# Moving eight of the tail's 36 extraction matmuls into the pauses of the last sums, and decode steps behind the last masks, in a top-10 kernel

## The chip, the cores and the metric

The kernel runs on one core of one Trainium2 chip. The metric is the device time of one execution in microseconds (us). Other words used below: TensorE is the matmul engine (PE in the profile, its weight loads PEld), VectorE is DVE, ScalarE is ACT, GpSimd is POOL, SyncE is SP. "Granted clock" is the share of TensorE's full clock that the throttle let through. A "pass" is one matmul of the profile in the extraction; an "ending" is the kernel's tail, from A (in the table below) on.

## The reference

```python
def reference(x, k):                      # x: [8192, 8192] float32, k = 10
    indices = np.argpartition(x, -k, axis=1)[:, -k:]
    values = np.take_along_axis(x, indices, axis=1)
    sorted_idx = np.argsort(-values, axis=1)
    return np.take_along_axis(indices, sorted_idx, axis=1)   # int64 [8192, 10]
```

## The kernel before

There are 64 tiles of 128 rows. For each tile ScalarE writes e = exp(36(x - 4.7)) in bf16, TensorE sums e into column groups (`s`, in PSUM), VectorE finds the 16 groups with the largest sums ("choose"), GpSimd gathers the candidates of 12 of them ("gather"), VectorE and GpSimd each spread half of the candidates into a masked square ("mask"), TensorE moves them to the right rows with 12 small fp32 matmuls ("extract"; each is two passes in the profile, so 24 passes a tile), and VectorE ranks them. Every few tiles a batch is decoded into column numbers: `slot`, `low`, `hot`, `pick`, `val` on VectorE, then `rows`, which places the values for the row moves on TensorE (`fo`). For all batches but one the rows are written by VectorE; for the last but one, ScalarE writes them with 16 instructions.

The parts that the change and the argument touch (cut):

```python
    def choose_steps(t):
        ...
        early = t >= last - 1            # the last two tiles gather in two halves
        return [
            lambda: nc.vector.max(out=w16[:, 0:8], in_=m),
            lambda: nc.vector.max_index(out=cid[:, 0:8], in_max=w16[:, 0:8], in_values=m),
        ] + ([lambda: index(0, G // 2), lambda: gather(t, 0, G // 2)] if early else []) + [
            lambda: nc.vector.match_replace(out=m2, ...),
            lambda: nc.vector.max(out=w16[:, 8:16], in_=m2),
            lambda: nc.vector.max_index(out=cid[:, 8:16], ...),
        ] + ([lambda: index(G // 2, G), lambda: gather(t, G // 2, G)] if early
             else [lambda: index(0, G)])

    def mask(eng, t, g0, g1):            # two SBUF inputs, 128x768 for half a tile
        eng.tensor_tensor(out=masked[t][:, g0:g1], in0=cands[t][:, g0:g1]..., in1=layout(t).own..., op=ALU.mult)

    def extract(t, c0=0, c1=G):
        for c in range(c0, c1):
            nc.tensor.matmul(gs[t][:, c * R:(c + 1) * R], lhsT=masked[t][:, c]..., rhs=layout(t).place)

    def finish_steps(b):
        ...
        return [slot, low, hot, hot_times_cid, pick, val, spread_rows] + moves + [copy_out, dma_out]   # named here for short

        # the tail: a, b, c are the last three tiles; wc holds the sums' steps of c
        mask(nc.gpsimd, a, G // 2, G)
        run(choose_steps(b))
        mask(nc.vector, a, 0, G // 2)
        run(wc[4:])                      # the last four sums of c, with pauses for ScalarE
        run(later[1:])
        extract(a)                       # then three extractions without a pause
        run(rank_steps(a - 1))
        steps = finish_steps(batch_of[a - 1])
        run(steps[:4])
        mask(nc.gpsimd, b, G // 2, G)
        chosen = choose_steps(c)
        run(chosen[:4])
        mask(nc.vector, b, 0, G // 2)
        run(chosen[4:])
        extract(b)
        run(steps[4:7])                  # pick, val, rows of the last-but-one batch
        mask(nc.vector, c, 0, G // 2)
        extract(c, 0, G // 2)
        ...                              # good: a check of the sums
        run(rank_steps(a))
        mask(nc.vector, c, G // 2, G)
        extract(c, G // 2, G)
        run(steps[7:])                   # the row moves on TensorE
        run(rank_steps(b)); run(rank_steps(c))
        ...
        run(finish_steps(batch_of[last]))
```

## Time and profile before

| | us |
|---|---|
| three timed runs | 678.6, 679.62, 681.07 |
| profiled run | 680.31 (span on the core 678.5) |
| last exponential on ScalarE ends ("A") | 653.22 from the start of the span |
| maximum over the last sums starts on VectorE ("T") | 653.98 |
| last extraction pass ends on TensorE | 669.12 |
| last rows start on VectorE | 673.16 |

The prediction below shows the lines that carry its reading. Two things help with them. A line of the chain of waits is "start, us, what", and each was released by the one above it or by its own engine's order. In a timeline the number in brackets at the end is the engine's idle time before the group and what ended it. And one more view of before, which the prediction did not show, will matter: the timeline of VectorE ahead of the last rows.

```profile
669.15 0.37 DVE L282 MAX8 t8a<-g 128x8 f32<-128x192 f32 x1 [3.23 <-PE g L269]
...
672.86 0.19 DVE L351 SCALAR_TENSOR_TENSOR val<-low,pick 128x30 f32<-128x30 uint16 x1
673.16 0.41 DVE L317 TENSOR_TENSOR rows<-val,cpack 128x240 f32<-128x240 f32 x1
```

VectorE idles 3.23 us until TensorE has finished the extraction of c, then ranks and decodes c without a stop up to the rows. So in the kernel before the rows start 4.04 us after the last extraction pass (673.16 - 669.12) because of VectorE's own steps. The row moves on TensorE lie beside that and are done by 672.50.

### The profile page before, as it was taken

To read this page: it belongs to the slowest core of one execution; us is meant where nothing else is said; L and a number is where in the kernel's file an instruction comes from. 1 tells how busy PE (TensorE), PEld (TensorE's weight loads), DVE (VectorE), ACT (ScalarE), POOL (GpSimd) and SP (SyncE) were. 2 spreads that over 40 slices of the span, in tenths; PEclk is the share of its full clock that TensorE was granted. 3 is DMA by queue.
4 is the path that set the end of the run, shared out by engine and by line. 5 is a ranking of instruction groups with operands and counts; after the bars stand their busy time and mean duration, and the time that the engine had idled before them with its cause. 6 is when DMAs were issued, how large, how long until landed. Compare 5 with 4: busy or idle time off the path is not lost.

```text
span 678.5 us, 7906 instructions
## 1 busy us (share of the span) xinstructions
PE 549.6 (81%) x2645; PEld 343.8 (51%) x2690; DVE 552.9 (81%) x1272; ACT 495.3 (73%) x295; POOL 180.0 (27%) x136
## 2 busy tenths in 40 slices
PE   1488877887978988877987888897988988877977
PEld 0146544555634555653753555553555555554656
DVE  3568878789868988789787897888977899879985
ACT  4777777777777777776777777687777777778851
POOL 0113223313313223313322313322331322331330
PEclk9867987859866777798787685976788768788875
DMA  8999999999999999999999999999999999999910
GB/s 354 420 421 420 419 421 419 421 419 421 419 421 420 421 418 420 421 419 420 420 421 420 420 419 421 420 419 421 419 420 418 421 417 415 418 420 398 405 49 7
DMA packets 73712, 269.77 MB, mean 398 GB/s; under 512 B 4398, under 2 KB 5062, under 8 KB 73670
## 3 DMA queue, kind: packets, MB, share of 16 engines
q1 hardware_dynamic: 72976, 268.54, 97.0%
q10 hardware_dynamic: 694, 0.71, 0.3%
q8 instruction: 21, 0.34, 0.2%
q14 instruction: 21, 0.17, 0.1%
HBM read 268.58 MB, written 0.66 MB: 397 GB/s over the span
## 4 chain that ended last, share of the span: by engine, by line
DMA 61%; PE 12%; SPq 7%; ACT 7%; issue 5%; DVE 5%; POOL 3%; ACTq 0%; DVEq 0%
DMA xt<-in_x_dram 59%; SPq L115 7%; ACT e L181 7%; PE s L188 6%; PE g L269 5%; POOL cand L235 3%; DMA out_dram<-opack 2%; DVE wall L222 1%; PE fo L333 1%; DVE cidb L228 1%; DVE cidb L223 1%; DVE m L225 1%; DVE wall L227 1%; DVE masked L252 0%; DVE pick L350 0%
## 5 line engine op out<-in xcount | busy, mean ns | idle before, releaser
L181 ACT ACTIVATE e<-xt,bias 128x4096 bf16<-128x4096 f32 (+2 forms) x138 | 477.6, 3461 | 153.4 <-DMA xt<-in_x_dram 136.4
L188 PE MATMUL s<-e,group 128*128 128x512 bf16 x979 | 334.6, 496 | 122.1 <-ACT e L181 117.6
L188 PEld LDWEIGHTS <-group 128*128 128x128 bf16 x1024 | 122.1, 122 | 309.5 <-issue 254.0
L269 PEld LDWEIGHTS g<-cpack,masked 128*128 128x128 f32 x1536 | 210.7, 217 | 17.9 <-issue 5.8
L269 PE MATMUL g<-cpack,masked 128*128 128x8 f32 (+1 forms) x1536 | 202.7, 272 | 2.0 <-DVE masked L252 1.7
L235 POOL INDIRECT_COPY cand<-xt,idx 128x192 f32 (+1 forms) x66 | 65.9, 998 | 476.3 <-DMA xt<-in_x_dram 129.1
L222 DVE MAX8 wall<-s 128x8 f32<-128x1024 f32 (+1 forms) x64 | 77.2, 1206 | 113.9 <-PE s L188 105.2
L252 POOL TENSOR_TENSOR masked<-cand,cpack 128x768 f32<-128x768 f32 x63 | 113.2, 1797 | 5.2
L223 DVE FIND_INDEX8 cidb<-wall,s 128x8 uint16<-128x1024 f32 (+1 forms) x64 | 76.7, 1198 | 0.0
L228 DVE FIND_INDEX8 cidb<-wall,m 128x8 uint16<-128x1024 f32 (+1 forms) x64 | 76.4, 1193 | 0.0
L225 DVE MATCH_REPLACE8 m<-wall,s 128x1024 f32<-128x1024 f32 (+1 forms) x64 | 76.1, 1189 | 0.0
L227 DVE MAX8 wall<-m 128x8 f32<-128x1024 f32 (+1 forms) x64 | 75.8, 1184 | 0.2
L252 DVE TENSOR_TENSOR masked<-cand,cpack 128x768 f32<-128x768 f32 x65 | 61.8, 951 | 0.0
L333 PE MATMUL fo<-rows,send 128*64 128x160 f32 (+3 forms) x128 | 27.8, 366 | 1.1 <-DVE rows L317 1.1
L181 ACT ACTIVATION_READ_ACCUMULATOR e<-xt,bias 128x1 f32 x138 | 25.7, 186 | 0.0
L333 PEld LDWEIGHTS fo<-rows,send 128*64 128x64 f32 (+2 forms) x128 | 18.1, 159 | 3.3 <-DVE rows L317 1.7
L282 DVE MAX8 t8a<-g 128x8 f32<-128x96 f32 (+1 forms) x64 | 16.2, 253 | 3.3 <-PE g L269 3.2
L285 DVE FIND_INDEX8 posb<-t8a,g 128x8 uint16<-128x96 f32 (+1 forms) x64 | 16.7, 260 | 0.0
L287 DVE FIND_INDEX8 posb<-tall,g 128x8 uint16<-128x96 f32 (+1 forms) x64 | 16.4, 257 | 0.0
L283 DVE MATCH_REPLACE8 g<-t8a,g 128x96 f32<-128x96 f32 (+1 forms) x64 | 16.1, 252 | 0.0
L214 DVE TENSOR_SCALAR idx<-cidb,cpack 128x12 uint16<-128x12 uint16 (+1 forms) x66 | 15.6, 237 | 0.2
L286 DVE MAX8 tall<-g 128x8 f32<-128x96 f32 (+1 forms) x64 | 15.8, 247 | 0.0
(38 smaller groups left out, 85.8 us busy)
## 6 DMA issues: line engine op xcount, KB each, us to landing
xt<-in_x_dram SPq DMA_DIRECT2D x248, 1024.0 KB, 16.0
xt<-in_x_dram SPq DMA_DIRECT2D x15, 512.0 KB, 9.1
xt<-in_x_dram SPq DMA_DIRECT2D x2, 256.0 KB, 10.1
out_dram<-opack ACTq DMA_DIRECT2D x6, 80.0 KB, 5.1
cpack<-topk_cpack ACTq DMA_DIRECT2D x1, 141.0 KB
out_dram<-opack ACTq DMA_DIRECT2D x1, 70.0 KB
out_dram<-opack SPq DMA_DIRECT2D x1, 60.0 KB, 1.7
out_dram<-opack SPq DMA_DIRECT2D x1, 30.0 KB, 1.5
```

Of the source, the lines that this page charges most:

```text
L115: nc.sync.dma_start(out=dst[:, s:s + n, :], in_=src[:, s:s + n, :])
L181: nc.scalar.activation(out=e, in_=xts[t][:, s0 * W:(s0 + n) * W], func=ACTF.Exp, bias=bias[:, 0:1], scale=BETA, accum_out=eall[:, first_su ...
L188: nc.tensor.matmul(sums[:, j:j + BANK], lhsT=lay.group[:, s0 + i, :], rhs=e[:, i * W + j:i * W + j + BANK], start=s0 + i == 0, stop=s0 + i ...
L222: lambda: nc.vector.max(out=w16[:, 0:8], in_=m),
L223: lambda: nc.vector.max_index(out=cid[:, 0:8], in_max=w16[:, 0:8], in_values=m),
L225: lambda: nc.vector.match_replace(out=m2, in_to_replace=w16[:, 0:8], in_values=m, imm_value=-1.0),
L227: lambda: nc.vector.max(out=w16[:, 8:16], in_=m2),
L228: lambda: nc.vector.max_index(out=cid[:, 8:16], in_max=w16[:, 8:16], in_values=m2),
L235: nc.gpsimd.add_instruction(mybir.InstIndirectCopy(name=nc.get_next_instruction_name(), ins=[nc.gpsimd.lower_ap(xts[t]), nc.gpsimd.lower_a ...
L252: eng.tensor_tensor(out=masked[t][:, g0:g1], in0=cands[t][:, g0:g1].unsqueeze(2).to_broadcast(shape), in1=layout(t).own.rearrange("p (c s) ...
L269: nc.tensor.matmul(gs[t][:, c * R:(c + 1) * R], lhsT=masked[t][:, c, :, :].rearrange("p a s -> p (a s)"), rhs=layout(t).place, start=True, ...
L333: nc.tensor.matmul(fo, lhsT=lay.send[:, i, 0:n * S], rhs=rows[:, i].rearrange("p a k -> p (a k)"), start=i == 0, stop=i == n - 1)
```

## The change

The intent: (1) do 8 of the 12 extraction matmuls of a in the pauses between the last four sums, where TensorE waits for ScalarE, and not behind them; (2) put the first mask of b ahead of the last choice, where VectorE is idle; (3) keep the second mask of c from waiting behind decode steps that are not yet needed: `val` and ScalarE's `rows` go behind it. The diff is whole:

```diff
@@ -403,28 +403,30 @@
         mask(nc.gpsimd, a, G // 2, G)
         run(choose_steps(b))
         mask(nc.vector, a, 0, G // 2)
-        run(wc[4:])
+        done = 0
+        for i, n in ((4, 3), (5, 3), (6, 2), (7, 4)):
+            run(wc[i:i + 1])
+            extract(a, done, done + n)
+            done += n
 
         run(later[1:])
-        extract(a)
         run(rank_steps(a - 1))
         steps = finish_steps(batch_of[a - 1])
         run(steps[:4])
         mask(nc.gpsimd, b, G // 2, G)
-        chosen = choose_steps(c)
-        run(chosen[:4])
         mask(nc.vector, b, 0, G // 2)
-        run(chosen[4:])
         extract(b)
-        run(steps[4:7])
+        run(choose_steps(c))
         mask(nc.vector, c, 0, G // 2)
         extract(c, 0, G // 2)
+        run(rank_steps(a))
+        run(steps[4:5])
+        mask(nc.vector, c, G // 2, G)
+        extract(c, G // 2, G)
+        run(steps[5:7])
         nc.vector.tensor_scalar(
             out=good[:, 0:nsums], in0=eall, scalar1=FINITE, scalar2=None, op0=ALU.is_lt,
         )
-        run(rank_steps(a))
-        mask(nc.vector, c, G // 2, G)
-        extract(c, G // 2, G)
         run(steps[7:])
         run(rank_steps(b))
         run(rank_steps(c))
```

## The prediction

> **What bounds the kernel now.** I read the page first, then the chain of waits, then the timeline and the stretch table of the last 30 us, because the diff touches nothing but the code for the last three tiles (a, b, c in the source). The page:
>
> ```profile
> span 678.5 us, 7906 instructions
> ...
> PEclk9867987859866777798787685976788768788875
> DMA  8999999999999999999999999999999999999910
> ...
> DMA 61%; PE 12%; SPq 7%; ACT 7%; issue 5%; DVE 5%; POOL 3%; ACTq 0%; DVEq 0%
> ```
>
> The DMA engines are full for all but the last 34 us (two slices of 17 us); they stream x and the change leaves them alone. So only the part after the last bytes, about 651 to 678 us, can move. The end of the chain that ended last, in order of time (start, us, what):
>
> ```profile
> 653.36 0.58 PE s L188
> 653.94 15.17 PE g L269 x72
> 669.12 3.38 PE fo L333 x12
> ...
> 672.52 0.30 ACT opack L330
> ...
> 673.16 0.42 DVE rows L317
> ...
> 673.62 1.05 PE fo L333 x6
> ```
>
> TensorE sets the end: after the last sums it does three extractions without a pause (72 passes; an fp32 matmul of the source is two passes, 36 matmuls), then the row moves of the last-but-one batch (12 passes). The last rows on VectorE start at 673.16, and what follows is fixed: 5.3 us to the end of the span. So I forecast one number, when those rows start. The stretch table (us, busy of PE, PEld, DVE, ACT, POOL, then granted clock, DMA share, GB/s), with stretches cut where the clock changes:
>
> ```profile
> 646.50:649.91 3.41, 1.88 (x8) 0.58 (x7) 3.29 (x10) 3.33 (x7) 1.12 (x2) 1.00 0.11 43
> 649.91:653.32 3.41, 1.74 (x6) 0.48 (x5) 2.25 (x8) 3.36 (x8) 0.81 (x2) 1.00 0.09 34
> 653.32:656.74 3.42, 3.38 (x16) 3.29 (x16) 2.69 (x7) 0.00 (x0) 2.14 (x2) 0.50 0.00 0
> 656.74:660.15 3.41, 3.41 (x18) 3.41 (x18) 3.27 (x7) 0.00 (x0) 0.93 (x1) 0.50 0.00 0
> ```
>
> The clock is full until 653.32 and half to the end, although TensorE is then never idle. A pass of the extraction costs 15.38/72 = 0.214 us there. At full clock it cost 1.41/12 = 0.118 us:
>
> ```profile
> 641.54 1.41 PEld L269 LDWEIGHTS g<-cpack,masked 128*128 128x128 f32 x12 [0.49 <-DVE masked L252]
> ```
>
> The pauses that the change fills, and the other engines' steps that could become the path (timelines of PE, POOL, ACT):
>
> ```profile
> 650.67 0.59 PE L188 MATMUL s<-e,group 128*128 128x512 bf16 x2 [0.58 <-ACT e L181]
> 651.95 1.08 PE L188 MATMUL s<-e,group 128*128 128x512 bf16 x3 [0.69 <-ACT e L181]
> 653.36 0.58 PE L188 MATMUL s<-e,group 128*128 128x512 bf16 x1 [0.33 <-ACT e L181]
> ...
> 657.95 0.93 POOL L235 INDIRECT_COPY cand<-xt,idx 128x96 f32 x1 [2.40 <-DVE m L225]
> 661.56 0.64 POOL L235 INDIRECT_COPY cand<-xt,idx 128x96 f32 x1 [2.68 <-DVE masked L252]
> ...
> 660.32 3.88 ACT L322 ACTIVATE rows<-val,cpack 128x60 f32<-128x60 f32 x16 [7.01 <-DVE val L351]
> ```
>
> ScalarE writes the rows for the last-but-one batch by 664.2, and TensorE uses them at 669.05: 4.8 us of slack in the kernel before.
>
> [...]every change of the clock in it lies on one grid of 3.413 us, the last at 653.32. [...]this trace says that the fp32 extraction counts for little, since 100% busy stretches of it stay at 0.50. [...]Measured is 118 ns at full and 214 ns at half clock; [...] Here the gather starts 2.2 and 2.5 us after the index it needs (655.75 to 657.95, 659.07 to 661.56), so a half gather really costs 2.2+0.93 = 3.1 us; I use that.
>
> **The change part by part.** Call T the moment when VectorE's maximum over the last sums starts (653.98 before).
>
> 1. Eight of the 12 extraction matmuls of a (16 of 72 passes) move between the last sums: 6 passes after the first, 6 after the second, 4 after the third. At half clock that takes 16 x 0.214 = 3.4 us off the work behind the sums. At full clock 6 passes are 0.71 us, and the first pause (651.10 to 651.95) holds them. The second group ends at 653.09, past the arrival of the third sum (652.66), and the third group at about 653.8 to 654.1, past the last sum (653.36). So the last sum comes late: T becomes about 654.2 at full clock, 654.75 where the clock falls at 653.3. Cost: 0.2 to 0.8 us of T.
>
> 2. The first mask of b (0.95 us) goes ahead of c's choice, into a gap of VectorE (idle 1.72 us before T). Its gather ended at 650.5, and the semaphore value it waits for is that gather alone, so it does not wait for the second. c's choice is then 0.95 us shorter, but the second gather of c stands behind the first on GpSimd: the first ends at T+1.77+3.13 = T+4.9, the second at about T+8.1. I expect no gain from this on the path.
>
> 3. Decode steps go behind the masks. VectorE: first mask of c at T+4.95 to T+5.9; ranks of a (1.8, before 661.22 to 663.02) to T+7.75; pick 0.93 to T+8.7; second mask of c (0.95) to T+9.7; val 0.38 only now, T+10.1 (before: 660.29, which is T+6.3).
>
> 4. TensorE at half clock, from T = 654.75: 8 passes of a to 656.3, 24 of b to 661.4, 12 of c (mask ready 660.7) to 664.0, the last 12 after the second mask (664.45) to 667.0. That is 2.1 us before the 669.12 of now; 3.4 minus 0.85 for the late sum and 0.45 for the mask.
>
> 5. The row moves need ScalarE's 16 instructions (3.88), which start after val: T+10.1 to T+14.0 = 668.75. TensorE waits 1.7 us. Then 12 passes, 3.44: T+17.45 = 672.2. VectorE's own chain for c (ranks 1.9 and decode to val 2.0 after 667.05) is done by 671.1, and its rows reuse the buffer that those moves read, so they wait for them. Rows of c start at 672.2 instead of 673.16: a gain of 0.95 us. With the clock held full a window longer (T = 654.2), 671.7: 1.4 us.
>
> **Sum.** 2.1 us saved on TensorE, of which 0.95 to 1.4 us arrives, because slack of 4.8 us in the rows becomes a wait. The profiled run took 680.31 us, so the like run after is 678.9 to 679.4.
>
> **Rivals.** (A) TensorE stays the bound and its 2.1 to 2.6 us arrive in full: about 677.5. For it: it is the bound now. Against: val moved from T+6.3 to T+10.1. (B) The clock decides. [...]at full clock the 56 passes left cost 0.118 instead of 0.214. In windows of this trace with five sums' matmuls and no extraction the clock fell each time; with 10 to 21 extraction passes among them it mostly stayed. So the filled pauses may hold the full clock for one more window. That shortens TensorE by up to 2.5 us, yet after the change the path runs over GpSimd, VectorE and ScalarE, so only T gains 0.5. The kernel before could gain up to 2.5 from a lucky phase, which is my reading of its spread (678.6 to 681.07); the one after less, as its path depends less on the clock. (C) An early fall of the clock, at 651.5, makes the 16 passes in the pauses cost 3.4 us in front of the last sum: T about 656, rows at 673.4, no gain or a small loss: 680.5. Against: [...]the extra passes work against a fall.
>
> **Range and chances.** Weighting the cases: TensorE-bound 677.5 (15%), the wait for the rows 678.9 to 679.4 (60%), no gain or a loss 680 to 680.5 (25%) gives about 679.1. The median before, 679.62, already lies 0.7 under the profiled run, so the expected step is small: I take 678.9 us, range 677.5 to 680.6, which also holds the 1.2 us that single runs scatter. Two per cent would be 13.6 us; all the work behind the sums is 25 us and the change moves 3.4 of it, so faster or slower by 2% are near impossible.
>
> **What would show it.** Right: 16 extraction passes between the last four sums; the maximum over the last sums 0.2 to 0.8 us later; the second c mask after the second gather and after pick; ScalarE's 16 row instructions near 664.5 to 668.5; TensorE idle 1 to 2 us ahead of the 12 row moves, released by ScalarE; the last rows at 671.7 to 672.3. Wrong: no idle ahead of those moves (rival A), T later than 655.5 (rival C), or the first b mask waiting for the second gather of b, which would delay T to 654.9 by itself.

The sum: it came to 2.1 us saved on TensorE, of which 0.95 to 1.4 us arrives, so 678.9 to 679.4 us for the like run, and 678.9 us as the point. Its figures are measured in the trace of before: the 118 and 214 ns are of one extraction pass (1.41 us for 12 loads, 15.38 us for 72 passes), the 2.2 and 2.5 us lie between the index and its gather. "In it" means the trace of before: its 96 recorded changes of the clock lie on one grid of 3.413 us to within 0.001 us. A "window" is one step of this grid. Of the windows at full clock that rival B speaks of, by the matmuls that start in them, those with five sums alone were followed by half clock in 3 of 3 cases, and those with five sums and 13 to 21 extraction passes by full clock in 3 of 5, so "mostly" rests on little.

## The result, and the profile after

| | runs (us) | median |
|---|---|---|
| before | 678.6, 681.07, 679.62, 680.31 | 679.96 |
| after | 677.34, 678.82, 677.9, 678.81 | 678.36 |

The ratio of after to before is 0.9975, with a 95% interval of 0.9952 to 0.9998. A ratio here is the mean time of one kernel's fast runs over that of the other's of the same rounds, so it is not quite the ratio of the medians. By the 2% measure the two are the same. The point predicted, 678.9, is 0.5 above the median after, and the range holds all four runs but the fastest. The same kernel before was run 24 more times beside the experiments; all 28 runs have a mean of 679.06 (677.42 to 681.07), so the four above fell high: against all 28, the four runs after (mean 678.22) are 0.84 us faster, though these were not all on one chip.

The profiled run after took 677.34, 3.0 us less than the profiled run before. The page of after, two lines, and the end of its chain of waits (start, us, what):

```profile
span 675.5 us, 7951 instructions
...
PEclk9877887877876668887687685976788768887896
```

```profile
652.46 0.57 PE g L269 x6
...
653.25 0.35 PE g L269 x4
...
655.40 0.73 DVE idx L214
...
657.75 0.97 POOL cand L235
...
661.52 0.80 DVE pick L350
662.32 0.87 DVE masked L252
663.18 0.14 DVE val L351
...
663.35 3.88 ACT rows L322 x16
...
667.28 3.26 PE fo L333 x12
...
670.56 0.42 DVE rows L317
```

The chain of before was one block of 15.17 us of extraction. This one leaves TensorE after the last sums and goes by VectorE, GpSimd's gather, VectorE, ScalarE's rows, and comes back for the row moves only. The extraction passes of a (x6, x4) are seen between the sums. The stretch table of after (us, busy of PE, PEld, DVE, ACT, POOL, then granted clock, DMA share, GB/s), cut where the clock changes:

```profile
649.70:653.10 3.40, 2.70 (x20) 2.01 (x19) 3.29 (x11) 3.36 (x8) 0.64 (x1) 1.00 0.09 34
653.10:656.50 3.40, 3.20 (x29) 3.07 (x28) 2.56 (x6) 0.12 (x2) 2.27 (x2) 1.00 0.00 1
656.50:659.90 3.40, 2.22 (x12) 2.12 (x11) 3.15 (x7) 0.00 (x0) 0.96 (x1) 0.51 0.00 0
...
666.80:670.20 3.40, 2.92 (x11) 2.26 (x12) 2.88 (x12) 0.43 (x2) 0.00 (x0) 0.50 0.00 0
670.20:673.60 3.40, 1.13 (x10) 0.56 (x8) 1.33 (x5) 0.59 (x2) 0.00 (x0) 1.00 0.10 27
```

In before the clock fell at 653.3, that is A+0.1. Here the stretch to 653.10 is about as placed, but has 20 matmul records of PE instead of 6, and the clock holds for one window more, to A+3.4. It also comes back at 670.20, so that the last six row moves took 0.63 us and not 1.05. Out of the timelines of GpSimd, VectorE and TensorE:

```profile
654.58 1.54 POOL L252 TENSOR_TENSOR masked<-cand,cpack 128x768 f32<-128x768 f32 x1
...
655.40 0.74 DVE L214 TENSOR_SCALAR idx<-cidb,cpack 128x6 uint16<-128x6 uint16 x1
...
667.28 3.25 PE L333 MATMUL fo<-rows,send 128*48 128x160 f32 x12 [1.30 <-ACT rows L322]
```

TensorE waits 1.30 us for ScalarE's rows: the wait that the prediction names. And an instruction in the chain, the index for the first gather of c, took 0.74 us where it took 0.23 in before; it ended with GpSimd's mask of b (654.58 + 1.54 = 656.12), which runs 0.6 us later than in before (654.00). No loss from it is seen at the gather itself, which starts 3.88 us after T, and 3.97 in before.

How much of the 3.0 us is the change? With the times of the two traces counted from A, the rows start at A+19.94 before and at A+17.43 after, a difference of 2.5 us; the rest is mostly the clock in the last moves. But the clock fell 3.3 us later in one trace than in the other. The grid of 3.413 us lay alike in both (a grid point at A+0.1 in before, at A+0.0 in after), so here the later fall goes with the fuller window ahead of it, 20 matmul records and not 6. In other runs the grid lies elsewhere: the clock fell at A+1.6 in e1 and at A-1.0 in e3, and no number of steps of 3.413 us leads from A+0.1 to either. One trace of each cannot say what the change is worth then. The experiments are for this.

The record has one more hint, sorted out after the fact. Of the 24 further runs of before, the seven with the highest mean granted clock (0.779 to 0.792) took 677.42 to 678.02; the other 17 took 678.07 to 681.04. The two runs after with a high clock took 677.34 (0.781) and 677.90 (0.787), much the same as those seven; the two with a clock of 0.767 took 678.8. So in runs with a high clock no gain is to be seen, though two runs cannot settle it.

### The profile page after: what moved, and what is told of

It is laid out like the page before. It is cut to its first block, busy times and chain, and to the rows that moved or that the text cites. A ratio compares the mean times of both kernels' runs of the same rounds, so it can differ in the third digit from the quotient of the medians.

```text
span 675.5 us, 7951 instructions
## 1 busy us (share of the span) xinstructions
PE 549.0 (81%) x2690; PEld 338.4 (50%) x2690; DVE 553.4 (82%) x1272; ACT 495.3 (73%) x295; POOL 180.2 (27%) x136
## 4 chain that ended last, share of the span: by engine, by line
DMA 68%; SPq 9%; PE 7%; ACT 5%; issue 4%; POOL 3%; DVE 3%; ACTq 0%
DMA xt<-in_x_dram 68%; SPq L115 9%; PE s L188 4%; ACT e L181 4%; POOL cand L235 3%; PE g L269 2%; DVE wall L222 1%; DMA out_dram<-opack 1%; PE fo L333 1%; ACT rows L322 1%; DVE masked L252 0%; DVE cidb L223 0%; DVE wall L227 0%; DVE m L225 0%; DVE cidb L228 0%
## 5 line engine op out<-in xcount | busy, mean ns | idle before, releaser
L188 PE MATMUL s<-e,group 128*128 128x512 bf16 x1024 | 341.4, 495 | 117.3 <-ACT e L181 116.9
L269 PEld LDWEIGHTS g<-cpack,masked 128*128 128x128 f32 x1536 | 205.9, 213 | 20.3 <-DVE masked L252 6.6
L269 PE MATMUL g<-cpack,masked 128*128 128x8 f32 (+1 forms) x1536 | 197.9, 268 | 3.7 <-DVE masked L252 3.5
L287 DVE FIND_INDEX8 posb<-tall,g 128x8 uint16<-128x96 f32 (+1 forms) x64 | 16.5, 258 | 0.0
## 6 DMA issues: line engine op xcount, KB each, us to landing
xt<-in_x_dram SPq DMA_DIRECT2D x2, 256.0 KB, 10.1
```

Source lines behind the costliest of these rows:

```text
L188: nc.tensor.matmul(sums[:, j:j + BANK], lhsT=lay.group[:, s0 + i, :], rhs=e[:, i * W + j:i * W + j + BANK], start=s0 + i == 0, stop=s0 + i ...
```

## The experiments

**How they were built.** The gather instruction was not to be run again and was kept out of every experiment. In its place (the "stand-in" of the expectations) GpSimd reads the index, runs a few memsets, and adds to a strided piece of x: same tiles, same waits, about the same time, wrong candidates. So all experiment kernels give wrong results, and they are compared with a kernel before and a kernel after changed in the same way:

```diff
-        nc.gpsimd.add_instruction(mybir.InstIndirectCopy(...))
+        nc.gpsimd.tensor_scalar(out=seed[:, g0:g1], in0=idxs[t][:, g0:g1]..., scalar1=3.0, scalar2=None, op0=ALU.min)
+        for _ in range(9 if g1 - g0 == G else 5):
+            nc.gpsimd.memset(filler, 0.0)          # 128x256
+        nc.gpsimd.tensor_tensor(out=cands[t][:, g0:g1], in0=seed[:, g0:g1], in1=xts[t]..., op=ALU.add)
```

Two theories were at stake. The wait theory (the prediction's): after the change the path runs over val and ScalarE's rows, so the time behind T hardly depends on the clock, and the gain is what TensorE's path lost minus that wait. The clock theory: what moved the time is that the filled pauses keep the full clock for another window, and the moved work and the new order matter little. Its rival half is the loss: passes in the pauses at half clock delay the last sum.

**c1: is the substitute for the gather good enough?** First setting, kernel before, with 6 memsets (3 for a half).

> Calibration, not a test of a theory. The real gather of GpSimd may not be run again, so every experiment uses the kernel before or after with a stand-in for it: GpSimd reads the same index and the same x tile, spends some time on memsets, and writes the same candidate tile (wrong values, same order, same semaphores). The stand-in should take from the index to the written candidates what the real gather took: 5.2 us for a whole one (index to end) and 3.1 us for a half one. I expect this first setting (6 and 3 memsets of 256 columns) to be within 2 us of that, the outputs to be wrong, and the whole kernel to take 675 to 685 us, since the stream of x still bounds it. [...]

One run took 680.05 us, the real kernel before on the same chip 678.02 (one run each). By its trace the substitute was too short: GpSimd spent 1.9 to 2.6 us on half a gather, and the real one takes 3.1 from the index to its end. So GpSimd ran ahead, and its mask of b took 2.30 us beside VectorE's work, and not 1.54 as in before. So the memsets were raised to 9 and 5 for all that follows.

**e1 to e4: the kernel before, the kernel after, part 1 and the rest of the change alone** (one chip, five rounds and the profiled run). e1 is before and e2 is after, with the substitute. e3 is e1 with part 1 only:

```diff
-        run(wc[4:])
+        done = 0
+        for i, n in ((4, 3), (5, 3), (6, 2), (7, 4)):
+            run(wc[i:i + 1])
+            extract(a, done, done + n)
+            done += n
         run(later[1:])
-        extract(a)
```

and e4 is e2 with exactly this taken back, so with parts 2 and 3 only.

> The kernel before, with the stand-in for the gather at its final setting (9 memsets for a whole gather, 5 for a half one). It is the base of all comparisons. Expected: index to written candidates 5 to 5.4 us (whole) and 2.9 to 3.3 us (half); time within 0.3% of the real kernel before; chain of waits at the end through three extractions without a pause and then the 12 row moves, as in the real one; single runs scattered over 2 to 3 us[...].

> The whole change, with the stand-in. If the stand-in is good, it is 1.0 to 2.4 us below the stand-in of before (ratio 0.9965 to 0.9985), and TensorE waits 1 to 2 us for ScalarE's 16 row instructions ahead of the 12 row moves, as in the real one. If the gain were from something in the real gather, the ratio would be 1.000.

> Part 1 alone: 16 of the 72 passes between the last sums; the masks and the decode steps stay as in before. My theory: this part carries the gain, and the rest gives nearly nothing, because val is then early (ScalarE done by about T+10.3), the last mask comes at T+10.0 instead of T+9.3, TensorE ends the last extraction at T+12.7, the row moves follow without a wait, and the last rows start at T+16.6, against T+16.7 measured for the whole change. So within 0.5 us of the whole change. Rival (the order of masks and decode is needed for the gain): less than half of the whole change's gain. T is the start of the maximum over the last sums.

> Parts 2 and 3 alone: first mask of b ahead of the last choice, decode behind the last masks, the extraction of a in one piece after the last sum. My theory: TensorE has 72 passes after the last sum and stays the bound, ScalarE's rows are ready before it is done, so the time is that of the stand-in of before within 0.5 us. Rival: if masks were what the end waits for, it gains half or more of what the whole change gains.

| six runs each | mean (us) | standard deviation | lowest to highest | ratio to the real before, 95% |
|---|---|---|---|---|
| e1 before | 679.32 | 0.99 | 677.76 to 680.09 | 1.0009 (0.9993 to 1.0026) |
| e2 after | 678.47 | 1.89 | 676.92 to 681.52 | 0.9999 (0.9976 to 1.0022) |
| e3 pauses only | 680.10 | 2.38 | 677.59 to 683.76 | 1.0019 (0.9990 to 1.0048) |
| e4 order only | 679.12 | 1.11 | 677.24 to 680.07 | 1.0009 (0.9995 to 1.0024) |

e1 against the real kernel, 1.0009, says that the substitute keeps the time (its two half gathers of c took 3.4 and 2.7 us from index to end, a little outside the 2.9 to 3.3 expected). e2 is 0.85 us under e1, the size of the real difference, but with a standard error of 0.87 the four cannot be told apart by their totals. The traces say more, and are tabled below with those of the next runs. The expectations for the two halves both failed. e3 was to come within 0.5 us of e2, and its mean is 1.6 above it (standard error 1.2). In its profiled run the clock fell at A-1.0, so ten of its 16 passes in the pauses ran at half clock, the last sum was late, T came at A+2.19, and the rows at A+19.40, that is T+17.21 and not the T+16.6 expected. With the rest of the miss goes a wait that the expectation left out: done with the passes of a, TensorE stood idle until VectorE had made its first mask of b, which in the old order stands behind the first index of c.

```profile
655.59 1.73 PE L277 MATMUL g<-cpack,masked 128*128 128x16 f32 x8
658.61 10.39 PE L277 MATMUL g<-cpack,masked 128*128 128x16 f32 x48 [1.29 <-DVE masked L260]
```

In q3 below the same wait is 1.96 to 2.01 us. So by these traces part 1 needs the early mask of part 2; the two without part 3 were not run. e4 was to have its rows from ScalarE in good time, and TensorE to be the bound. In total it is indeed like e1 (0.2 us less), but in its trace, with the clock falling at A+3.9, TensorE waits 1.20 us for ScalarE's rows, as in after.

**q1 to q4: four endings in one run.** As one ending is 25 us of 680, a bench was made in which the same tail comes four times: four blocks of 16 tiles, so with four endings, the first load of a block waiting for the end of the block before, and the slow fallback for failed checks left out.

```diff
+        for block in range(4):
+            gate = tile_topk_indices_kernel(tc, x[block * rows:(block + 1) * rows, :], k, out[...], gate, kept, block)
...
+        if t == 0 and gate is not None:            # the first tile of a block waits for the gate
+            nc.vector.tensor_copy(out=dst[:, :, 0], in_=gate.to_broadcast([P, lay.S]))
```

q1, q2 and q3 are e1, e2 and e3 as such benches. q4 is q1 with matmuls that do nothing useful in the pauses: no work moved, no order changed, only TensorE kept busy.

```diff
-        run(wc[4:])
+        for i, n in ((4, 6), (5, 6), (6, 4), (7, 0)):
+            run(wc[i:i + 1])
+            for _ in range(n):                     # bf16, 192 columns, result thrown away
+                nc.tensor.matmul(gs[a], lhsT=thin.group[:, 0, :], rhs=flat[:, 0:G * thin.R])
```

> Test bench: [...]Here the 64 tiles are done as four blocks of 16, each with the same whole ending, and a block's first load waits for the end of the block before. So each execution holds four endings, at four places of the clock's 3.413 us grid, and its time moves by four times the change of one ending. The kernel before, with the stand-in gather. Expected: 780 to 900 us in all; in the trace the four endings differ by up to 2.5 us, shorter where the clock falls later: the last rows start 17 to 19.5 us after T (start of the maximum over the last sums).

> The whole change in the test bench. My theory (slack of the row instructions turned into a wait; path over GpSimd, VectorE, ScalarE): the last rows start at T+16.4 to T+17 in all four endings, whatever the clock, TensorE waits for ScalarE in each, and T is 0 to 1.5 us late where the clock falls before the last sum. Time 3 to 6 us below the test bench of before (0.8 to 1.5 us an ending). Rival (the change gains nothing and the first comparison was luck of the clock): within 1.5 us.

> Part 1 alone in the test bench. My theory: last rows at T+16.6 to T+17.2, with T as late as in the whole change; so 70 to 100% of the whole change's gain, and its time 0 to 2 us above the whole change's. Rival (the reordering carries the gain): at most a third of it. The single-ending run of this edit came out late in the mean (two executions of 682 to 684 us), which speaks for the rival or for an early fall of the clock.

> The kernel before with nothing moved, but 16 bf16 matmuls of 192 columns, whose result is thrown away, in the same three pauses. [...]Theory of the clock (rival B of the prediction): the clock falls 1.5 to 4.9 us after the last sum and no longer before it, the 72 passes run partly at full clock, and an ending is 0.8 to 2 us shorter, total 3 to 8 us below the test bench of before, as much as the whole change. Theory of the moved work alone: no gain, or a loss of up to 0.5 us an ending for the late last sum.

| one chip | mean (us) | standard deviation | runs | ratio to the real before |
|---|---|---|---|---|
| q1 before | 772.61 | 1.19 | 5 | 1.1375 (1.1356 to 1.1394) |
| q2 after | 772.78 | 2.98 | 6 | 1.1391 (1.1358 to 1.1424) |
| q3 pauses only | 773.31 | 3.03 | 6 | 1.1404 (1.1375 to 1.1432) |
| q4 before with idle matmuls | 770.58 | 1.04 | 6 | 1.1348 (1.1330 to 1.1367) |

I expected 3 to 6 us between q1 and q2; q2 came out 0.2 us the slower (standard error 1.3), and q2 and q3, whose pauses are filled with extraction, scatter two and a half times as much as q1. That expectation failed, and with it that of q3, a share of a gain that is not there (q1 itself came out below the 780 expected). The cause was looked for in the traces. First, what the endings have in common. All times from A; "clock falls" is where the granted clock goes from 1.0 to 0.5 for the last time before the rows.

| trace | clock falls | T | extraction ends | last rows start |
|---|---|---|---|---|
| before, real | 0.1 | 0.76 | 15.90 | 19.94 |
| e1 | 1.6 | 0.56 | 14.63 | 18.66 |
| q1, endings 1 to 3 | 1.9, 3.1, 3.3 | 0.99, 0.56, 0.56 | 14.28, 13.73, 13.72 | 18.32, 17.77, 17.76 |
| after, real | 3.4 | 0.74 | 12.85 | 17.43 |
| e2 | 3.5 | 0.74 | 12.56 | 17.33 |
| q2, endings 2 to 4 | 4.6, 4.4, 1.4 | 0.74, 0.88, 0.74 | 12.77, 12.96, 12.55 | 17.53, 17.73, 17.32 |
| q3 (pauses only), endings 1 to 4 | 4.0, 1.3, 4.3, 3.9 | 0.74 in each | 13.50, 13.90, 13.38, 13.55 | 17.54, 17.95, 17.42, 17.59 |
| e4 (order only) | 3.9 | 0.56 | 12.48 | 17.15 |
| q4, endings 1, 3, 4 | 3.2, 4.3, 4.3 | 0.62 in each | 13.78, 13.26, 13.27 | 17.82, 17.30, 17.30 |

Left out are the endings with a late T: the fourth of q1, the second of q4 and the first of q2, which are taken up below. Three readings follow.

- In the kernel before, the rows start 4.04 us after the extraction ends in every line, and they follow the clock: where it falls at 0.1 instead of 1.6 they are 1.28 us later, 0.85 us for each us. Between falls at 3.1 and 3.3 nothing more is won (17.77 and 17.76): the passes of a are then done, and TensorE waits 0.23 us for VectorE's mask of b. Where the clock falls later still, more is won again: q4, which has the order of before, has its rows at 17.30 with a fall at 4.3.
- In the kernel after, the rows start 16.57 to 16.85 us after T in every line, wherever the clock falls (1.4 to 4.6). This is the wait theory's claim; by the clock theory alone the rows should come earlier the later the clock falls, and they do not.
- So the gain depends on where the clock falls. With a fall at 3.3 and 3.5 it is 0.4 us (17.76 against 17.33). With a fall at 4.3 and later there is none: after has 17.53 and 17.73, and q4 with the order of before 17.30. With a fall at 1.4 it is about 1.5 (an estimate: the slope of before puts its rows at 18.83, after has 17.32). With a fall at 0.1 in before and 3.4 in after, 2.5. When the clock falls late the new order alone does better than the whole change (e4: 17.15, 0.6 under q1), as its last sum is not late. Where it falls early the filled pauses help (q3 at 1.3: 17.95, against an estimate of 18.92 from the slope).

q4 shows how much the clock is worth alone. Its timeline of TensorE and its stretch table, third ending:

```profile
554.73 0.66 PE L424 MATMUL g<-group 128*128 128x192 bf16 x6
...
557.25 2.75 PE L282 MATMUL g<-cpack,masked 128*128 128x16 f32 x24
```

```profile
554.30:557.70 3.40, 3.22 (x27) 2.45 (x27) 2.66 (x10) 2.62 (x6) 3.09 (x9) 1.00 0.11 40
557.70:561.10 3.40, 3.17 (x29) 3.11 (x29) 3.30 (x8) 0.00 (x0) 2.74 (x5) 1.00 0.02 5
561.10:564.50 3.40, 3.40 (x18) 3.40 (x17) 3.30 (x8) 0.78 (x4) 2.94 (x9) 0.50 0.00 0
```

With 16 idle matmuls in the pauses the 24 passes of a, all still behind the last sum, took 2.75 us, 0.115 each, at the full clock. The rows started at A+17.30 in two endings: as early as in the changed kernel, with none of its work moved. The four endings together gained 2.0 us on q1 (standard error 0.7), 0.5 each; the expectation was 3 to 8. So the clock is a cause of its own, and its share is of the order of the whole change's 0.84 us.

Now the scatter. The first ending of q2 had T at A+2.58 and the rows at A+19.15. The last sum was not late there (it ended at A+0.70). The next run shows the same.

**q5 to q7: the scatter, and a version with both remedies** (another chip). q5 is q2 again, the base for this set. q6 adds idle matmuls earlier, meant to keep the clock from falling before the pauses:

```diff
-        run(wc[0:4])
+        for i, n in ((0, 0), (1, 4), (2, 4), (3, 4)):
+            run(wc[i:i + 1])
+            spare(n)                               # n bf16 matmuls of 192 columns, thrown away
...
             run(wc[i:i + 1])
+            if i == 4:
+                spare(2)
```

q7 is q6 with val and ScalarE's rows moved ahead of the ranks of a, and these ranks split around the second mask of c, to take away TensorE's wait:

```diff
-        run(rank_steps(a))
-        run(steps[4:5])
+        run(steps[4:7])
+        ranks = rank_steps(a)
+        run(ranks[:3])
         mask(nc.vector, c, G // 2, G)
         extract(c, G // 2, G)
-        run(steps[5:7])
+        run(ranks[3:])
```

> The whole change in the test bench once more, as the base for the two that follow, on their chip and in their rounds. Executions scattered over 5 us or more as before (768.4 to 776.3). Theory (an early fall of the clock makes the passes in the pauses cost 0.214 us each ahead of the last sums): an ending with a late T (T over 1.5 us after ScalarE's last exponential while VectorE stands idle ahead of it) has a clock that fell before that exponential ended; from T on, the last rows come at T+16.5 to T+16.9 in every ending.

> The whole change plus 14 bf16 matmuls of 192 columns with a discarded result in the pauses after the second, third, fourth and fifth of the last sums, ahead of and among the extraction passes. [...]Theory (early falls are what eats the gain): no ending has its clock fall before the last sum, none has a late T for TensorE's sake, the scatter shrinks to 3 us or less, and the time is 1 to 4 us below the whole change's. Rival (the scatter is from the DMA or elsewhere): same scatter, and a time within 1 us of it, or above it for the added work.

> The same, and the decode up to val with ScalarE's rows moved ahead of the ranks of a, whose last two steps go behind the last mask. Theory (after the change the path runs over val and the 16 row instructions): TensorE no longer waits for ScalarE ahead of the 12 row moves, the last rows start at T+15.5 to T+15.9 instead of T+16.6, and the time is 3 to 4.5 us (four endings) below the one with held clock alone. Rival (TensorE or the second gather of c binds anyway): T+16.4 or later, and less than 1.5 us.

| six runs each | mean (us) | standard deviation | ratio to the real before |
|---|---|---|---|
| q5 after | 773.58 | 2.27 | 1.1390 (1.1360 to 1.1421) |
| q6 clock held | 772.67 | 2.85 | 1.1384 (1.1351 to 1.1416) |
| q7 held, and val early | 771.85 | 3.08 | 1.1363 (1.1325 to 1.1401) |

The expectation of q5 looked for late T with VectorE idle and an early fall of the clock. Its two endings with a late T (A+2.53, A+3.06) are not of that kind, as VectorE was busy up to T in both and the clock fell after A; its other claim, rows at T+16.5 to T+16.9, held (16.57 to 16.64). q6 tested whether early falls of the clock make the scatter. Nothing speaks for it, and its rival fits better: it is 0.9 us under q5 (standard error 1.5), not 1 to 4, and its runs span 7 us, not 3; its profiled run has no late T (0.74 to 0.97 in all endings, rows 17.33 to 17.70), but its six runs scatter as much as those of q5. What the trace of q5 shows instead, in its fourth ending (A = 747.40), in the timelines of TensorE, GpSimd and VectorE:

```profile
747.73 0.38 PE L195 MATMUL s<-e,group 128*128 128x512 bf16 x1
...
748.01 1.71 POOL L265 TENSOR_TENSOR masked<-cand,cpack 128x768 f32<-128x768 f32 x1
...
748.25 2.29 DVE L265 TENSOR_TENSOR masked<-cand,cpack 128x768 f32<-128x768 f32 x1
750.46 0.69 DVE L229 MAX8 wall<-s 128x8 f32<-128x512 f32 x1
```

The last sum was there at 748.1, but the maximum over it started at 750.46. VectorE was late by its own earlier steps, and the first mask of b, which the change puts ahead of the choice, met GpSimd's mask of b and took 2.29 us instead of 0.95. GpSimd's mask ends at 749.72, and VectorE's, which started 0.24 us behind it, 0.82 us later: about its own length of 0.95, as if it had done little until GpSimd's was through. That is read from the ends alone; why the two slow each other is not shown. The other order is there too: in the third ending of q5 VectorE's mask started 0.03 us after the substitute's own add on GpSimd, ended 0.83 us after that add's end and took 1.23, and GpSimd's mask, which started behind it, took 2.14 instead of 1.54. Such meetings are in one ending of q2, two of q5 and three of q7; in all of them T is at A+2.53 to A+4.59. In before, this mask stands behind the first index of c, when GpSimd's is done, and takes 0.95 in all four endings of q1.

Two cautions. The bench makes VectorE late: its blocks have 16 tiles, and q1 and q4 each have one ending with T at A+3.23 and A+3.51 without any such meeting. And the substitute lets GpSimd's mask start earlier (A+0.36 in e2) than the real gather does (A+1.45 in the real trace after, where VectorE's mask had ended at A-0.04). So the meeting is shown for the bench. That it happens in the real kernel, or made the slow run of e2 (681.52), is not shown, as no trace of a slow run was taken. Nor can it be the whole scatter: e3 and q3 leave this mask where it was in before, no ending of q3 has a meeting, and yet they scatter as much (683.76 in e3; standard deviation 3.03 in q3). What makes the scatter stays open.

q7 did what it was built for in every ending: the rows start 15.38 to 15.61 us after T, 1.2 less than in after. The timelines of ScalarE and TensorE, third ending (A = 554.09):

```profile
563.46 3.88 ACT L335 ACTIVATE rows<-val,cpack 128x60 f32<-128x60 f32 x16 [9.28 <-DVE val L364]
...
568.08 3.08 PE L346 MATMUL fo<-rows,send 128*48 128x160 f32 x12
```

ScalarE is done at 567.34, 0.7 us before TensorE needs the rows, and the wait in front of the row moves is gone. With it the rows start again 4.04 us after the end of the extraction, as in before. In totals q7 is only 0.8 us under q6 (standard error 1.7), where 3 to 4.5 were expected, and 1.7 us under q5, 0.4 an ending, with a standard error of 1.6, so this is not settled; and as the gather could not be run in it, there is no version with right results that is shown to beat both kernels.

## Why the prediction was right or wrong, point by point

- **Size and class.** Right: 678.9 predicted, 678.36 measured, within 2%. Some of it is luck. The like run was to take 678.9 to 679.4 and took 677.34, below the range's end of 677.5; the last rows were to start at 671.7 to 672.3 and started at 670.56. What came after them was called fixed at 5.3 us and took 4.9, as the clock came back. The median fits because two of the four runs after, with a mean clock of 0.767, took 678.8.
- **Slack of the rows becomes a wait (step 5).** Right. TensorE idled 1.30 us in front of the row moves (predicted 1.7), released by ScalarE, and rows minus T stays within 0.3 us over all its endings. From A, ScalarE was done 3.1 us later than before (14.09 against 10.98) and TensorE 3.05 earlier (its extraction ends at 12.85 against 15.90); together that is 6.15, 1.3 more than the slack of 4.85 (669.05 less 664.20). The terms of the path were a little smaller than predicted: T to ScalarE's first row 9.48 us (predicted 10.1), then 3.88 for the rows, 0.05 until TensorE starts and 3.28 for the moves; 16.69 and not 17.45 in sum. The gathers began 1.61 and 2.28 us after their index, under the 2.2 and 2.5 taken from before.
- **The last sum comes late (step 1).** Right in mechanism, and in size if counted from endings at full clock. T did not move between the two profiled runs (A+0.76, A+0.74), but only because two things cancel: the passes put the last sum off by 0.18 us (its start, A+0.14 and A+0.32), and the sum itself ran at full clock in after (0.38 us) and at half in before (0.58). In endings of before with the clock full, T is at A+0.56 (e1, q1); with the passes it is at A+0.74 (e2, q3), 0.18 later, where 0.2 was predicted. With the clock fallen at A-1.0 (e3) T came at A+2.19: rival C's mechanism is real.
- **The slope of the kernel before.** Rival B says that before could win up to 2.5 us from a lucky phase: measured, 2.18 between a fall at 0.1 (the real kernel) and at 3.3 (the bench) (19.94 and 17.76).
- **The path of before.** One detail of the first part was wrong without harm. It put the row moves between the extraction and the last rows, as the chain of waits lists them. VectorE's timeline shows ranks and decode of c there, and the moves beside them, 0.66 us short of the path. Both start with the end of the extraction, so the sum did not suffer.
- **"The one after less."** Wrong. The prediction expected less spread of the changed kernel as its path no longer hangs on the clock. Behind T that is so. But T itself now hangs on more: passes at half clock in front of the last sum (e3: T at A+2.19), and a mask that can meet GpSimd's (q2, q5, q7: T at A+2.53 to A+4.59). These do not explain all of it (q3). In the six runs each of e1 and e2 the standard deviation is 0.99 and 1.89, in q1 and q2 1.19 and 2.98. The four real runs after spread less (0.73), too few to say.
- **Step 2 saw "no gain" in the early mask, and no loss.** Both were missed. The gain: step 4 lets the passes of b follow those of a at 656.3, which needs this mask early. Where it stays in its old place, TensorE waits 1.29 to 2.01 us for it (e3, q3). The loss: GpSimd's mask of b ran 0.6 us later and met the index, which took 0.74 instead of 0.23; in the real trace this is not seen at the gather (T+3.88, before T+3.97), in the bench the two endings of q2 with an index of 0.44 and 0.50 have their rows at T+16.80 and T+16.85 and not T+16.58. And in the bench the mask itself took up to 1.3 us more in the endings with such a meeting (2.29 and not 0.95). What the mask's move alone does was not run. Why GpSimd's second gather of b began 0.65 us later (653.76 against 653.11) stays open; the trace puts the end of its wait down to VectorE's early mask (652.14 to 653.09), which is inferred.

So of the 3.0 us between the two profiled runs, the endings say that where the clock falls at the same place the change brings from nothing (a fall at 4.3) over 0.4 us (3.3 to 3.5) to some 1.5 (1.4, an estimate); the rest goes with a clock that falls later, and in this pair, with the grid in the same place, the filled pauses are the likely reason, as idle matmuls hold the clock too (q4: it fell at A+3.2 to A+4.3, in q1 at A+1.9 to A+3.3). What that makes in an average run is not settled by the totals: e1 and e2 differ by 0.85 with a standard error of 0.87, q1 and q2 not at all.

## What to carry to other kernels

A tail of 25 us is timed here against a clock that changes on its own grid of 3.413 us (falls from A-1.0 in e3 to A+4.6 in q2): compare endings with the clock falling at the same place, or change only the clock (idle matmuls in the pauses) to see its share, before a gain is put down to moved work. Taking work off the engine that sets the end pays until the slack of the next path is used up, so work out that slack first (here 4.85 us in the rows, against 6.15 that the change took from it). Work taken off that engine is also won only if its next input is there (here the mask of b). And a mask on VectorE that is moved into a gap should be looked at against what GpSimd does then (here 2.29 us instead of 0.95 beside GpSimd's mask), also in runs where one of the two is late.

## What the traces show of the clock, the passes, the gather and the masks

- All changes of the clock in the traces of before and after lie on a grid of 3.413 us (96 and 102 recorded changes, to within 0.001 us), and its values are 0.50 and 1.00 only. Which work lets the clock rise or stay is shown in part: fp32 extraction with 16 columns did not raise the clock though TensorE was busy 3.38 to 3.41 of 3.41 us in a window (0.50 from 653.3 on in before), while a window with 11 records of row moves of 160 columns, busy 2.92 of 3.40, was followed by full clock (666.8 to 670.2 in after; a like window of q6, with 10 records, was not). In the trace of before, windows at full clock with five recorded sums of 512 columns and nothing else were followed by half clock (3 of 3), those with seven or more by full clock (10 of 10); other traces have a few exceptions each way (in q4 and q5 one with seven, in q6 one with five); with 16 bf16 matmuls of 192 columns in the pauses it stayed full to A+3.2 to A+4.3 in the four endings of q4 (A+1.9 to A+3.3 without them, in q1).
- An extraction pass, with one load of 128x128 weights each, took 118 ns at full clock (1.41 us for 12 loads) and 214 ns at half clock (15.38 us for 72 passes), both in before.
- The gather began 1.61 to 2.5 us after the index it needed (2.20 and 2.49 in before, 1.61 and 2.28 in after).
- A 128x768 fp32 mask on VectorE took 2.29 us instead of 0.95 behind GpSimd's mask (q2, q5). A 128x6 index took 0.74 instead of 0.23, ending 0.02 us after GpSimd's mask (after); what held it is not shown.
